# Layer 0's MLP: down products with the features on the partitions, and what follows from it

## The chip, the cores and the metric

One core of one Trainium2 chip runs the whole program. The metric is the device time of one execution in microseconds. Three runs of the kernel before gave 1023.16, 1023.51 and 1023.9 (median 1023.51).

## What is computed

Two layers of an encoder on x of 512 tokens by 1024 features, all in float32:

```
for layer in 0, 1:
    h = rms_norm(x, norm_mix[layer])
    x = x + (stick_breaking_attention(h) if layer == 0 else rglru_block(h))
    h = rms_norm(x, norm_mlp[layer])
    u = relu(h @ w1[layer])           # 512 x 4096
    x = x + (u * u) @ w2[layer]       # 512 x 1024
return rms_norm(x, norm_final)
```

The change concerns the second product of layer 0's MLP, called the down product, and the step from it to the first product of layer 1's mixer (`rglru_block`, weights `w_in`).

## The kernel before

**Layout.** Between the stages x lies transposed: eight chunks `x[c]` of 128 features (on the partitions) by 512 tokens. The chunks 0 to 3 are one half of the features, 4 to 7 the other.

**Exact products.** Every product is made of three: each operand is split into a high half (a cast to fp32r) and a low half (operand minus high half, also fp32r), and high times high, high times low and low times high are added up in PSUM. So each weight that arrives costs a cast on ScalarE (ACT), `wh`, and a subtraction on VectorE (DVE), `wl`. `halves` (L132 on) does the same for x times the norm's gain, into `xgh` and `xgl`.

**The MLP (class `Mlp`).** The 4096 hidden features are taken in four quarters. `quarters` first makes 1024 hidden features by plain products (`squared`); `run` then works through the list `steps`: 14 down steps for the first quarter, and for each further quarter 14 up steps and 14 down steps. Both use seven products of half-size blocks in place of eight (Winograd's scheme): `PRODUCTS` names them P1 to P7, with the block of the left operand, the block of weights, the block that is added to it before, the PSUM sum, the output quadrant and its sign. The order of the down steps is `ORDERS["mid"]`: P1 0, P5 0, P1 1, P2 0, P5 1, P6 0, P6 1, P3 0, P3 1, P7 0, P7 1, P2 1, P4 0, P4 1; the digit is the half of the quarter. In this document these are steps 0 to 13. Layer 1's MLP is the `mixed` one; layer 0's isn't.

**A down step before** (`part`, matmuls on L1190): the squared hidden values are the stationary operand (128 tokens), the weights move (512 features), so a PSUM bank holds 128 tokens by 512 features. There are 12 matmuls, first the 8 with `wh`, then the 4 with `wl`. `collect` takes a sum out of PSUM into a quadrant `c[out]`, multiplied on the way by the token's norm factor, which is one number per partition (`rr`, L1158). The quadrants: c0 and c1 belong to the first 256 tokens, c2 and c3 to the last 256; c0 and c2 to features 0 to 511, c1 and c3 to the others. P1 and P2 go into c0, P6 and P3 into c1, P4 into c2, P5 and P7 into c3, over all quarters.

**The end before.** `end` makes P4 of the last quarter by `times` (L1149). `feature` (L1518 on) turns a chunk back by four 128x128 transposes on TensorE (L1522) into PSUM, adds it to x (`add_x`, L765) and makes `xgh` and `xgl`. Chunks 4 to 7 come after the first half of P4, chunks 0 to 3 inside `beside`, which makes the first two `w_in` products. `Squares` gathers the squares for the next norm.

**What sets the order.** TensorE (PE) runs strictly in the order of the program. The other engines and the queues are ordered by a scheduler, except where the class `Ordered` wraps an engine: each instruction then comes after the one before it (`issue_after`). `Mlp` wraps V (DVE) and A (ACT), not G (GpSimd, POOL). All of these record L793. `prepare` makes the weights of a step about four steps ahead: `leave(i)`, called as the program comes to step i + 1, first collects the sum that step i completed, then prepares step i + 4. `operand` (L1109) makes `wh` and `wl`; there are four buffers of each, so a step's buffers are those of the step four earlier. `added` (L1127) makes the sums of weight blocks: P5 and P6 mostly on DVE, P7 and P4 by a transfer that adds in flight, issued on POOL's queue (L1131). In `operand`, UP_AT and OPEN_AT are small offsets in a buffer's row.

`x` itself is put away to DRAM while its tiles serve other ends (`between`), and `back` loads it again on SP's queue (L1547) as the last quarter's down steps begin.

The functions that the diff touches:

Of the kernel before, what the change touches and what calls it, by code (L numbers as in the profile page):

```python
# [18 lines left out]
P = 128  # L19
# [45 lines left out]
def hybrid_encoder(  # L65
# [81 lines left out]
    class Squares:  # L147
# [4 lines left out]

        def chunk(self, c, xc, last=None, pool=None, e=V):
            if not self.begun:
                self.begun = True
                self.acc = work.tile([P, S], F32, tag="r", name="ssq")
                A.activation(self.acc, xc, AF.Square)
            else:
                sq = (pool or work).tile([P, S], F32, tag="sq", name="sq")
                A.activation(sq, xc, AF.Square)  # L160
                with tc.issue_after(last.ins) if last else nullcontext():
                    self.last = e.tensor_tensor(self.acc, self.acc, sq, ALU.add)
# [640 lines left out]
    class Mlp:  # L803
# [323 lines left out]
        def added(self, unit, name, far=False):  # L1127

            _, b, to, *_ = self.PRODUCTS[name]
            if far or name in self.FAR:  # L1130
                G.dma_start(  # L1131
                    out=unit[b].rearrange("p j n -> p (j n)"), in_=unit["src"](to), accum_op=ALU.add
                )
# [41 lines left out]
        def part(self, sums, name, g, w):  # L1175
# [8 lines left out]
            if (name, g) == ("P1", 1):  # L1184
                rounds = ((h, wh),), ((h, wl),), ((l, wh),)
            for n, pairs in enumerate(rounds):
                for i in range(2):
# [13 lines left out]
        def run(self, first, between, end):  # L1201
# [42 lines left out]
            def make(i):  # L1244
# [3 lines left out]
                kind, q4, p, name = steps[i]  # L1248
                at = 0
                if kind == "up":  # L1250
                    at = self.OPEN_AT if i == 0 or (p, name) == (0, "P1") else UP_AT
                ws[i] = made[i] = self.operand(self.source(unit(i), name), at)

# [59 lines left out]
            def leave(i):  # L1313
# [5 lines left out]
                if kind == "down":  # L1319
# [124 lines left out]
            for i, (kind, q4, g, name) in enumerate(steps):  # L1444
# [12 lines left out]
                if new:  # L1457
                    banks[to] = self.bank()
                self.up(name, ws.pop(i), banks[to], new)
            for e in (self.V, self.A):  # L1460
                e.turn(False)
            end([ws[len(steps) - 2 + g] for g in range(2)], sums["down", NQ - 1, 0]["X"])

# [19 lines left out]
        def quarters(self, between, end):  # L1483
            for c in range(C - 1):
# [13 lines left out]
                if c == C - 2:  # L1498
                    self.rr = self.sq.inv_squares(self.bank())
                between(c)  # L1500

# [8 lines left out]
    with ExitStack() as mctx:  # L1510
# [6 lines left out]

        def feature(c, tag):  # L1518

            pt = bank(tag)  # L1520
            for t in range(NB):
                PE.transpose(  # L1522
                    pt[:, t * P : (t + 1) * P], mlp.y(t, c // 4)[:, c % 4 * P : (c % 4 + 1) * P],
                    ident,
                )
            add_x(c, pt)
            last["low"] = halves("mix1", c, x[c])
# [15 lines left out]

        def back():
            for c in range(C):
                x[c] = home_tile(*HOMES[c], "x")
                nc.sync.dma_start(out=x[c], in_=away[:, c, :])  # L1547

        end.ready = back
# [464 lines left out]
```

## Time and profile before

| | |
|---|---|
| median of three runs | 1023.51 us |
| the profiled execution | 1023.47 us |
| its span on the core | 1021.7 us |
| granted clock of TensorE, mean | 0.998 |
| the last quarter's down steps up to P4 | 520 to 552.7 us of the span |
| there: PE, DVE, ACT, POOL busy | 32.70, 31.25, 19.80, 3.49 us of 32.7 |
| P4, transposes and two `w_in` products | 552.7 to 572.5 us |
| there: PE, DVE, ACT, POOL busy | 19.80, 17.56, 13.56, 4.72 us of 19.8 |
| transfers of 512 KB that add, on POOL's queue | 66 in the MLPs, 10 in layer 1's mixer |

Times in rows are microseconds from the span's start; a row of a timeline has the start, the length, the engine, the line, the operation, what it writes and reads, and the count. In brackets stands the idle time before it and what ended it. The ends of matmuls are modelled, so the pace of PE is read from the starts. A row of the waits names the engine, who it waited for, the sum, the count and the longest. Issue to landing is counted from the start of the issuing instruction.

### The profile page before, as it was taken

Reading aid. Unit: us, or ns where it says so; the run is one execution under the profiler, and the core shown is the slowest. Engines: PE = TensorE matmul, PEld = TensorE weight load, DVE = VectorE, ACT = ScalarE, POOL = GpSimd, SP = SyncE. Lnnn points to the kernel's source line nnn. Section 1 sums busy time; section 2 is a strip of 40 time slices with the busy share of each in tenths; the row PEclk is TensorE's granted clock in tenths of the full one; section 3 lists DMA queues with packets and bytes.
Section 4 is the critical chain, followed back from the end, with each engine's and each line's share of the span. In section 5 each row is a group of like instructions: output and inputs, shape, how many; then the busy total and the mean of one; then the engine's idle time right before and its main releaser. Section 6 shows DMA issues by size and latency. Waiting matters only on the chain.

```text
span 1021.7 us, 16053 instructions
## 1 busy us (share of the span) xinstructions
PE 1013.0 (99%) x5930; PEld 890.1 (87%) x5930; DVE 868.3 (85%) x1165; ACT 701.5 (69%) x1081; POOL 175.5 (17%) x239
## 2 busy tenths in 40 slices
PE   9999999999999999999999999999999999999997
PEld 8888888888888988988988888888988988988986
DVE  7988787848789799799799888899898898898897
ACT  7777676835767764764775799966873763873866
POOL 0454344420000011011011221100010010010012
PEclk9999999999999999999999999999999999999999
DMA  7745454537536666676783476446767667667653
GB/s 237 222 122 145 115 152 102 152 111 262 160 81 198 166 156 195 166 158 194 166 230 90 118 192 173 116 170 200 214 112 206 165 143 202 173 142 201 168 106 111
DMA packets 58719, 165.73 MB, mean 162 GB/s; under 512 B 6928, under 2 KB 12304, under 8 KB 58640
## 3 DMA queue, kind: packets, MB, share of 16 engines
q1 hardware_dynamic: 47264, 124.41, 37.5%
q0 software_dynamic: 10944, 39.85, 23.4%
q8 instruction: 47, 0.77, 0.3%
q10 hardware_dynamic: 432, 0.44, 0.1%
q14 instruction: 32, 0.26, 0.1%
HBM read 140.56 MB, written 6.29 MB: 144 GB/s over the span
## 4 chain that ended last, share of the span: by engine, by line
PE 93%; ACT 3%; DVE 2%; DMA 1%; issue 1%; POOL 0%; ACTq 0%; DVEq 0%
PE ps_t L1190 16%; PE ps_acc L1055 9%; PE ps_acc L1190 9%; PE ps_z L1055 8%; PE ps_acc L234 5%; PE ps_acc L236 5%; PE ps_acc L235 5%; PE ps_o L1055 5%; PE ps_z L1190 4%; PE ps_t L234 2%; PE ps_t L236 2%; PE ps_t L235 2%; PE ps_o L234 2%; PE ps_o L236 2%; PE ps_o L235 2%; PE ps_t L628 2%
## 5 line engine op out<-in xcount | busy, mean ns | idle before, releaser
L793 ACT CAST wh<-b 128x1024 fp32r<-128x1024 f32 x174 | 180.3, 1051 | 121.6 <-DVE b L793 76.7
L793 DVE TENSOR_TENSOR wl<-b,wh 128x1024 fp32r<-128x1024 f32 x174 | 210.4, 1220 | 38.7 <-ACT wh L793 37.5
L1131 POOL DMA_DIRECT2D b<-in_w_dn x40 | 35.0, 875 | 295.3 <-DVE b L793 198.6
L234 PE MATMUL ps_acc<-xgh,wh 128*128 128x512 f32 x192 | 78.4, 408 | 0.0
L793 ACT ACTIVATE u<-u 128x512 f32<-128x512 f32 x103 | 64.9, 632 | 15.3 <-DVE u L793 13.5
L236 PE MATMUL ps_acc<-xgl,wh 128*128 128x512 f32 x192 | 75.2, 392 | 0.0
L235 PE MATMUL ps_acc<-xgh,wl 128*128 128x512 f32 x192 | 75.1, 391 | 0.0
L1131 POOL DMA_DIRECT2D b<-in_w_up x26 | 22.7, 872 | 291.7 <-DVE b L793 100.7
L606 DVE TENSOR_TENSOR_SCAN scan<-keep,later 128x128 f32<-128x128 f32 (+1 forms) x64 | 58.7, 918 | 15.4 <-POOL w L600 7.6
L793 DVE TENSOR_TENSOR b<-b,b 128x1024 f32<-128x1024 f32 x50 | 61.2, 1224 | 1.3
L610 POOL TENSOR_TENSOR w<-w,scan 128x128 f32<-128x128 f32 (+1 forms) x64 | 53.0, 830 | 53.4 <-DVE scan L606 48.8
L793 DVE TENSOR_TENSOR u<-u 128x512 f32<-128x512 f32 (+1 forms) x89 | 55.0, 618 | 4.4 <-ACT u L793 2.5
L229 DVE TENSOR_TENSOR wl<-raw,wh 128x512 fp32r<-128x512 f32 (+2 forms) x64 | 54.3, 877 | 4.1 <-ACT wh L227 4.0
L793 ACT CAST wh<-raw 128x1024 fp32r<-128x1024 f32 x49 | 51.2, 1048 | 6.8 <-PE ps_acc L1190 2.9
L227 ACT CAST wh<-raw 128x512 fp32r<-128x512 f32 (+2 forms) x64 | 44.4, 732 | 14.8 <-PE ps_acc L236 7.3
L1055 PE MATMUL ps_z<-xgh,wh 128*128 128x256 f32 x216 | 50.6, 277 | 0.2
L793 DVE TENSOR_TENSOR wl<-raw,wh 128x1024 fp32r<-128x1024 f32 x39 | 48.0, 1230 | 0.8 <-ACT wh L793 0.8
L1190 PE MATMUL ps_t<-wh,bh 128*128 128x512 f32 x120 | 47.0, 392 | 0.0
L1190 PE MATMUL ps_t<-wh,bl 128*128 128x512 f32 x120 | 46.8, 390 | 0.0
L600 POOL TENSOR_SCALAR_AFFINE_SELECT w<-w 128x128 f32<-128x128 f32 x64 | 32.9, 513 | 69.9 <-ACT w L595 69.7
L1055 PE MATMUL ps_acc<-low,wh 128*128 128x256 f32 x192 | 44.7, 276 | 0.0
L793 DVE TENSOR_TENSOR sl<-u,sh 128x512 fp32r<-128x512 f32 (+2 forms) x53 | 37.9, 716 | 7.7 <-ACT sh L793 7.7
(419 smaller groups left out, 3215.9 us busy)
## 6 DMA issues: line engine op xcount, KB each, us to landing
b<-in_w_dn SPq DMA_DIRECT2D x48, 512.0 KB, 4.3
b<-in_w_dn POOLq DMA_DIRECT2D x40, 512.0 KB, 5.6
b<-in_w_up SPq DMA_DIRECT2D x39, 512.0 KB, 4.6
b<-in_w_up POOLq DMA_DIRECT2D x26, 512.0 KB, 5.5
raw<-in_w_dn SPq DMA_DIRECT2D x16, 512.0 KB, 4.6
raw<-in_w_in SPq DMA_DIRECT2D x16, 512.0 KB, 3.7
raw<-in_w_up SPq DMA_DIRECT2D x13, 512.0 KB, 4.0
raw<-in_w_qk SPq DMA_DIRECT2D x12, 512.0 KB, 3.8
```

What stands on the lines that cost most here:

```text
L227: e[0].copy(wh[:, k, :], raw[:, k, :])
L229: e[1].tensor_tensor(wl[:, k, :], raw[:, k, :], f(wh[:, k, :]), ALU.subtract)
L234: PE.matmul(ps, wh, ah, start=start, stop=False)
L235: PE.matmul(ps, wl, ah, start=False, stop=False)
L236: PE.matmul(ps, wh, al, start=False, stop=stop)
L600: G.affine_select(t, t, pattern=[[-1, P]], compare_op=ALU.is_gt, fill=0.0, base=0, channel_multiplier=1,)
L606: V.tensor_tensor_scan(sc[:, S - n : S][:, ::-1], keep[:, :n][:, ::-1], later[:, S - n :][:, ::-1], 1.0, ALU.mult, ALU.max,)
L610: G.tensor_tensor(wt, wt, sc[:, S - n + 1 : S + 1], ALU.mult)
L793: ins = getattr(self.e, name)(*args, **kwargs)
L1055: PE.matmul(ps[:, i * HS : (i + 1) * HS], m, y, start=new and i == k == low == 0 and y is h, stop=(low, i, k) == steps[-1], skip_group_che ...
L1131: G.dma_start(out=unit[b].rearrange("p j n -> p (j n)"), in_=unit["src"](to), accum_op=ALU.add)
L1190: PE.matmul(sums[to][i], a[:, j, block, i * P : (i + 1) * P], y[:, j, :], start=new and g == j == n == 0 and a is h, stop=g == j == 1 and ...
```

## The change

For layer 0's MLP only:

- The down products are made by features (`across`, in `part` and at the end): the weights are the stationary operand (128 features), the squared hidden values move (256 tokens). A step is 24 matmuls of 256 columns, 16 with `wh`, then 8 with `wl`. The quadrants now hold two times 512 columns: for each 128 features, 256 tokens. So no transposes are needed. The offsets of the weights in their buffers change with their role.
- A token's factor is now different along the row. `collect` adds or subtracts without a factor; each quadrant is multiplied once, when its last sum is in, by a tile `rr` that holds the 512 factors on every partition. The factors are stored to DRAM (`keep_factors`) and loaded back, spread to all partitions, with x (`back`). The multiplications are on DVE (`times_factors`); P4's last sums are multiplied in PSUM.
- c2 (as it stands after P6) and c1 (after P3) are added to x by four transfers each, of 128 KB, that add in flight, on POOL's queue (`block`). c3 and c0, and P4's sums, are added by DVE.
- In the last quarter the low halves of six steps' weights (`ADDED`: steps 8 to 13) are no longer subtracted on DVE: ACT writes minus the high half into `wl`, and a transfer on POOL's queue adds the raw weights to it.
- GpSimd's transfers of layer 0's MLP are wrapped by `Ordered` as well, so they are issued in the order of the program.
- The operations after P4 (high and low halves of x, squares) are written out in a fixed order on DVE and ACT; the squares go through the ordered ACT.

The core of the diff:

```diff
-            self.V, self.A = Ordered(V), Ordered(A)
+            self.V, self.A, self.G = Ordered(V), Ordered(A), Ordered(G)
+            self.G.turn(not self.mixed)
...
+        ADDED = (("P7", 0), ("P7", 1), ("P3", 1), ("P2", 1), ("P4", 0), ("P4", 1))
+
-        def operand(self, raw, at):
+        def operand(self, raw, at, added=False):
...
             self.A.copy(wh, raw)
-            self.V.tensor_tensor(wl, raw, f(wh), ALU.subtract)
+            if added:
+                self.A.activation(wl, f(wh), AF.Copy, scale=-1.0)
+                self.G.dma_start(out=wl, in_=raw, accum_op=ALU.add)
+            else:
+                self.V.tensor_tensor(wl, raw, f(wh), ALU.subtract)
             return wh, wl
...
-                G.dma_start(
+                self.G.dma_start(
                     out=unit[b].rearrange("p j n -> p (j n)"), in_=unit["src"](to), accum_op=ALU.add
                 )
...
+        def across(self, name, g, i, w, ps, new=False, ends=True, rounds=None):
+
+            block = self.PRODUCTS[name][0]
+            (wh, wl), (h, l) = w, self.a[g]
+            rounds = rounds or [((h, wh), (l, wh)), ((h, wl),)]
+            for n, pairs in enumerate(rounds):
+                for jj in range(2):
+                    for a, y in pairs:
+                        for k in range(2):
+                            f0 = (2 * i + k) * P
+                            PE.matmul(
+                                ps[:, k * HS : (k + 1) * HS], y[:, jj, f0 : f0 + P], a[:, jj, block, :],
+                                start=new and n == jj == k == 0 and a is h,
+                                stop=ends and (n, jj, k) == (len(rounds) - 1, 1, 1),
+                                skip_group_check=name not in ("P1", "P5", "P2"),
+                            )
...
+            if not self.mixed:
+                if (out, i) in self.begun:
+                    op = ALU.subtract if less else ALU.add
+                    self.gained = self.V.tensor_tensor(y, y, ps, op)
+                else:
+                    self.begun.add((out, i))
+                    A.activation(y, ps, AF.Identity, scale=1.0 - 2.0 * less)
+                return
...
+                added = kind == "down" and q4 == NQ - 1 and not self.mixed
+                ws[i] = made[i] = self.operand(
+                    self.source(unit(i), name), at, added and (name, p) in self.ADDED
+                )
...
                     if p:
                         for n in range(2):
                             self.collect(name, n, bank[n])
+                        if not self.mixed and q4 == NQ - 1:
+                            end.done(name)
                     if not ahead:
                         prepare_or_hold(i)
...
+        def block(out):
+            h, ts = out % 2, (lo, hi)[out // 2]
+            times_factors(mlp.V, mlp.c[out].rearrange("p i n -> p (i n)"), ts)
+            for k in range(4):
+                mlp.G.dma_start(
+                    out=x[4 * h + k][:, ts],
+                    in_=mlp.c[out][:, k // 2, k % 2 * HS : (k % 2 + 1) * HS], accum_op=ALU.add,
                 )
+        def done(name):
+            if name == "P6":
+                block(2)
+            elif name == "P3":
+                block(1)
+            elif name == "P7":
+                times_factors(mlp.V, mlp.c[3].rearrange("p i n -> p (i n)"), hi)
+            elif name == "P2":
+                add_block(mlp.V, 3)
+                times_factors(mlp.V, mlp.c[0].rearrange("p i n -> p (i n)"), lo)
...
         def end(ws, xs):
             for i in range(2):
                 for g in range(2):
-                    mlp.times("P4", g, i, ws[g], xs[i], False)
-                mlp.collect("P4", i, xs[i])
-                if i == 0:
-                    for c in range(4, C):
-                        feature(c, "zzoo"[c - 4])
-                        squares.chunk(c, x[c], e=G)
+                    mlp.across("P4", g, i, ws[g], xs[i], ends=g == 1)
...
+            high(4, 5, 6, 7)
+            low(4, 5)
+            add_block(mlp.V, 0, range(2))
+            low(6, 7)
+            square(4, 5)
+            times_factors(mlp.V, xs[0], hi)
+            add_last(0)
+            high(0)
+            square(6)
+            high(1)
+            times_factors(mlp.V, xs[1], hi)
+            add_block(mlp.V, 0, range(2, 4))
+            add_last(1)
+            low(0, 1)
+            square(7)
+            high(2, 3)
+            low(2, 3)
...
         beside(
-            [slab(w_in[C + i]) for i in range(2)], xgh, xgl, begin,
-            {
-                1: lambda: [feature(c, "z") for c in range(2)],
-                2: lambda: [feature(c, "o") for c in range(2, 4)],
-            },
-            (*range(4, C), *range(4)),
+            [slab(w_in[C + i]) for i in range(2)], xgh, xgl, begin, {}, (*range(4, C), *range(4)),
         )
```

`high` and `low` make `xgh` and `xgl` of chunks on the ordered ACT and DVE; `add_block` adds a quadrant's parts to x on DVE; `add_last` adds P4's sums.

More of the change, by code (lines that the diff above doesn't have):

```diff
@@ L1459, in run @@
                 self.up(name, ws.pop(i), banks[to], new)
+            rest = [ws[len(steps) - 2 + g] for g in range(2)], sums["down", NQ - 1, 0]["X"]
+            if not self.mixed:
+                end(*rest)
             for e in (self.V, self.A):
                 e.turn(False)
-            end([ws[len(steps) - 2 + g] for g in range(2)], sums["down", NQ - 1, 0]["X"])
+            if self.mixed:
+                end(*rest)
         def mixed_quarters(self, residues, gains, end):
@@ L1499, in quarters @@
                     self.rr = self.sq.inv_squares(self.bank())
+                    between.factors(self.rr)
                 between(c)
@@ L1516, in hybrid_encoder, with keep_factors @@
         last = {}
[L1518 to L1524, printed above, removed]
-                )
-            add_x(c, pt)
-            last["low"] = halves("mix1", c, x[c])
+        factors = dram.tile([1, S], F32, tag="factors", name="factors")
+        lo, hi = slice(0, HS), slice(HS, S)
+        rr = []
+        def keep_factors(cols):
+            nc.sync.dma_start(
+                out=factors.rearrange("o (t p) -> p (o t)", p=P), in_=cols[:, :NB]
+            )
@@ new lines, in back, with times_factors @@
+        def back():
+            for c in (*range(4), *range(4, C)):
+                x[c] = home_tile(*HOMES[c], "x")
+                nc.sync.dma_start(out=x[c], in_=away[:, c, :])
+                if c == 0:
+                    rr.append(mlp.mp.tile([P, S], F32, tag="low", name="rr", bufs=1))
+                    nc.sync.dma_start(out=rr[0], in_=factors.broadcast_to([P, S]))
+        def times_factors(e, y, ts):
+            n = y.shape[1] // HS
+            y = y.rearrange("p (k n) -> p k n", k=n)
+            e.tensor_tensor(y, y, rr[0][:, ts].unsqueeze(1).broadcast_to([P, n, HS]), ALU.mult)
@@ L1529, in end, with low, square @@
+        def low(*cs):
+            for c in cs:
+                last["low"] = mlp.V.scalar_tensor_tensor(
+                    xgl[:, c, :], x[c], col("mix1")[:, c : c + 1], f(xgh[:, c, :]),
+                    ALU.mult, ALU.subtract,
+                )
+        def square(*cs):
+            for c in cs:
+                squares.chunk(c, x[c], e=G, a=mlp.A)
         def end(ws, xs):
@@ L1542, in between @@
                 soft.send(mlp.ready)
[L1544 to L1549, printed above, removed]
+        between.factors = keep_factors
+        end.ready, end.done = back, done
         mlp.quarters(between, end)
```

33 lines of the change are left out of this document (27 added, 6 removed).

## Prediction

> **What bounds the kernel now.** I read the page's busy times first, then PE's waits, then the chain of waits around the end of layer 0, then the timelines of ACT, DVE, POOL and the DMA queues there. Page, part 1, and the whole list of PE's waits:
>
> ```profile
> PE 1013.0 (99%) x5930; PEld 890.1 (87%) x5930; DVE 868.3 (85%) x1165; ACT 701.5 (69%) x1081; POOL 175.5 (17%) x239
> PE ps_z L396 <- DVE dense_ones L118: 1.1, 1, 1.1
> PE ps_z L587 <- ACT keep L596: 0.2, 1, 0.2
> ```
>
> PE is never let wait: two waits, 1.3 us, in the whole span. So any matmul time taken out shortens the kernel, and any operand that comes late lengthens it, one for one. The chain at the end of layer 0's last down quarter (start, length, what):
>
> ```profile
> 517.23 2.72 PE ps_z L1055 x24
> 519.95 2.75 PE ps_t L1190 x12
> ...
> 550.02 2.72 PE ps_z L1190 x12
> 552.74 2.72 PE ps_t L1149 x12
> 555.46 0.87 PE ps_z L1522 x8
> 556.34 0.87 PE ps_o L1522 x8
> 557.21 2.75 PE ps_t L1149 x12
> 561.32 0.87 PE ps_z L1522 x8
> 563.58 0.87 PE ps_o L1522 x8
> ```
>
> Each of the fourteen down steps is 12 matmuls of 512 columns in 2.72 us (I number them 0 to 13: 8 is P3 1, 9 and 10 are P7 0 and 1, 11 is P2 1, 12 and 13 are P4 0 and 1). L1522 are the transposes.
>
> **Matmuls.** The change turns a step into 24 matmuls of 256 columns. The row of 24 (L1055, the up product) and the row of 12 both last 2.72 us, each matmul with a weight load of its own, so the price is nothing in the row. The Trainium skill, "TensorE: Matmul & The Clock Gate", section "Back-to-back issue gap", speaks against it: it gives the gap as N/2.4 + 2.5 ns, so 672 more matmuls (4 quarters x 14 steps x 12) would add an estimated 1.7 us; the trace's equal rows do not bear that out, and it stays out of the sum.
>
> **Transposes.** They go. Timeline of PE, the first matmul of step 8, of P4, and the first matmul after the two w_in products (48 matmuls of 512):
>
> ```profile
> 541.70 0.39 PE L1190 MATMUL ps_acc<-wh,sh 128*128 128x512 f32 x1
> 552.58 0.39 PE L1149 MATMUL ps_t<-wh,bh 128*128 128x512 f32 x1
> 572.50 0.39 PE L234 MATMUL ps_t<-xgh,wh 128*128 128x512 f32 x1
> ```
>
> 552.58 to 572.50 is 19.92 us; the 24 + 48 matmuls that stay need 72 x 2.72/12 = 16.32. Removed: 3.6 us, all of it on the path.
>
> **Row multiplications, adds and the end on DVE.** Collecting keeps its operations (one pair per product, 1.41 us below, now without a scale). New: four products by the factors, eight adds of 256 columns, the two last PSUM blocks; gone: eight adds of x, two collects, six low halves. Timeline of DVE (the 277.74 row is the price of a 256-column operation, the pitch of following ones 0.34):
>
> ```profile
> 277.74 0.42 DVE L793 TENSOR_TENSOR x<-x 128x256 f32<-128x256 f32 x1
> 278.08 0.42 DVE L793 TENSOR_TENSOR low<-x,s 128x256 fp32r<-128x256 f32 x1
> 537.97 1.41 DVE L793 SCALAR_TENSOR_TENSOR c<-ps_acc,rr,c 128x512 f32<-128x512 f32 x2
> 541.02 0.68 DVE L793 TENSOR_TENSOR sl<-u,sh 128x512 fp32r<-128x512 f32 x1
> 542.76 1.41 DVE L793 SCALAR_TENSOR_TENSOR c<-ps_t,rr,c 128x512 f32<-128x512 f32 x2
> 545.21 1.22 DVE L793 TENSOR_TENSOR wl<-raw,wh 128x1024 fp32r<-128x1024 f32 x1
> 546.35 1.41 DVE L793 SCALAR_TENSOR_TENSOR c<-ps_acc,rr,c 128x512 f32<-128x512 f32 x2
> 547.66 2.35 DVE L793 TENSOR_TENSOR wl<-b,wh 128x1024 fp32r<-128x1024 f32 x2
> 549.93 1.41 DVE L793 SCALAR_TENSOR_TENSOR c<-ps_t,rr,c 128x512 f32<-128x512 f32 x2
> ```
>
> If PE never stalled, it would reach chunk 0 of the w_in products at 552.58 + 5.44 + 5.44 = 563.5 and need its low half 0.45 later. Before that half DVE has, from 549.93: two collects (2.6), two products by the factors (2.3), the two w_in low halves (2.3), eight adds (2.7), two PSUM products (1.3), four PSUM adds (1.4), four low halves (2.6), by pitches 1.31, 1.14, 0.34 and 0.66: 15.2 us, and the half itself 0.75. That is 565.9, 2.0 us late. Where PE has stalled 2 us or more after step 10, this costs nothing; the next late thing is then the transfers.
>
> **The six low halves.** Now the wait that I think decides. A low half was one DVE operation straight after ACT's cast; now ACT casts, ACT writes the negative, and POOL issues a transfer that adds the raw weights. ACT around it, the negative's price from the same operation in layer 1's mixer, POOL's transfers of this kind there, and the last weight transfer ahead on POOL's queue with its landing:
>
> ```profile
> 534.60 2.00 ACT L793 CAST wh<-b 128x1024 fp32r<-128x1024 f32 x2 [4.01 <-DVE b L793]
> 536.51 0.61 ACT L793 CAST sh<-u 128x512 fp32r<-128x512 f32 x1
> 537.03 1.05 ACT L793 CAST wh<-b 128x1024 fp32r<-128x1024 f32 x1
> 578.56 1.06 ACT L793 ACTIVATE wl<-wh 128x1024 fp32r<-128x1024 f32 x1
> ```
> ```profile
> L1639 POOL DMA_DIRECT2D wl<-raw x10: 855/886/908, 580.0 to 650.6; - x10
> DMA to landing us min/median/max: 4.5/6.1/7.9
> ```
> ```profile
> 537.32 0.88 POOL L1131 DMA_DIRECT2D b<-in_w_dn  x1 [3.97 <-DVE wl L793]
> DMA to landing us min/median/max: 5.4/5.4/5.4
> ```
>
> The cast at 537.03 is step 8's; it can't come earlier, since ACT's order is written out and the two casts before it waited for DVE's sum (b in the first row), which the change leaves where it is. The negative ends near 539.0, the transfer is issued at 539.1. PE wants the low half two thirds into the step: 541.70 + 1.81 = 543.5. The fastest of ten landings gives 543.6, the median 545.2. So step 8 stalls by 0.1 to 1.7 at least, before any queueing.
>
> Queueing: two issues of the same quarter that follow each other on POOL's queue, each with its landing, and the page's two queues:
>
> ```profile
> L1131 POOL DMA_DIRECT2D b<-in_w_dn x1: 875/875/875, 518.4 to 518.4; - x1
> DMA to landing us min/median/max: 8.1/8.1/8.1
> L1131 POOL DMA_DIRECT2D b<-in_w_dn x1: 865/865/865, 520.7 to 520.7; - x1
> DMA to landing us min/median/max: 8.2/8.2/8.2
> q1 hardware_dynamic: 47264, 124.41, 37.5%
> q0 software_dynamic: 10944, 39.85, 23.4%
> ```
>
> They landed at 526.5 and 528.9, 2.4 apart. POOL's 39.85 MB took 23.4% of 16 engines' 1021.7 us: 3.15 us for 0.52 MB, against 1.6 on SP's queue. So adding transfers of 512 KB follow each other at 2.4 to 3.15 us, beside steps of 2.72, and the change puts six of them and eight of 128 KB (0.6 to 0.8 each, by bytes) into one line.
>
> POOL's order is now written out too. After step 6 DVE collects P6 and multiplies c2 (the collect, at 542.76 before, moves up, as two low halves of weights leave DVE ahead of it: from 537.97, a pair of 1.3 and two low halves of u at 0.6 end near 540.5, P6's pair near 541.7, the product by the factors near 542.8); then POOL issues four transfers to x, which at 0.88 each hold it until 546.3. ACT, at 1.0 for a cast or a negative and 0.5 for a sh, has step 9's negative at 541.4, which still goes ahead of them, and step 10's at 543.3, which is queued behind them. After P3, four more hold it from 548.8 to 552.3, and P4's two low halves are issued at 552.3 and 553.2.
>
> With the rule "4.5 us after issue, and no sooner than the spacing after the one before", starting from 542.7 (537.3 + 5.4), at spacing 2.4: step 8 lands at 545.1 (stall 1.6); step 9 at 547.5, wanted 546.2 + 1.6, none; the blocks at 549.9; step 10 at 552.3, wanted 548.95 + 1.6 (stall 1.75); step 11 in time; blocks 557.1; P4 0 at 559.5, wanted 553.5 + 3.35 (2.65); P4 1 at 561.9, wanted 554.85 + 6.0 (1.05): 7.1 us in all. At 3.15 the same walk gives 2.3, 0.45, 3.55, 0.45, 4.45 and 1.8: 13.0. I take the middle, 10.1, since the one spacing is a single pair and the other a mean with other traffic in it. DVE's end is then covered.
>
> **Small things at nothing.** The factors' store goes out on SP's queue in layer 0's first products, their broadcast with the reload of x ahead of the last down steps; both are first used after step 6. ACT's six negatives are in the issue times above. Layer 1's mixer starts from PE's stream and moves with it. The new offsets of the weights are those that the up products have, at full rate. If these covers fail: under 1 us together, either way.
>
> **The sum.** -3.6 + 10.1 = +6.5 on the profiled execution's 1023.47 us (span 1021.7 and 1.8 around it; median of the runs 1023.51): 1030.0, with 1026.9 to 1032.9 as this case's own range (-3.6 + 7.1 to -3.6 + 13.0).
>
> **Rivals.**
> - *The transfers land in time, so it is faster.* If an adding transfer needs at most 4.4 us, side by side with others, and a 128 KB one keeps POOL for a quarter of 0.88, then step 8 is met at 543.5, step 10's is issued at 543.7 and lands at 548.1 before 548.95, and P4's are early. Left are -3.6 and up to 2.0 for DVE's end: 1019.9 to 1021.9. For it: no transfer in the trace of before made PE wait. Against it: ten landings, none under 4.5. Here the Trainium skill, "DMA: Bandwidth & Descriptors", section "Anatomy of one DMA", stands on this side: 2.0 us + bytes/436e3 gives an estimated 3.2 us for 512 KB. The trace disagrees, 4.5 to 7.9. Chance 0.25 (0.2 of it beyond 0.2%).
> - *No queueing, only the order.* Each transfer takes its median 6.1 us and none delays another, POOL still works through its order: stalls of 1.7 at step 8, 1.8 at step 10 (issue 546.35), 1.4 at P4: 4.9 - 3.6 = +1.3, 1024.8. For it: engines often stand idle there. Against it: the pair 2.4 apart. Chance 0.2, of which 0.05 goes over 0.2%.
> - The forecast: 0.55.
>
> **The numbers.** A difference under 0.2% (2.05 us) can't be told from none by these runs. Faster 0.2, same 0.05 + 0.15 = 0.2, slower 0.55 + 0.05 = 0.6. The range reaches from inside the first rival to just above the forecast's upper end: 1020.5 to 1033.5, with about 0.1 left out on each side.
>
> **What would show it.** In the profile after: 24 matmuls of 256 columns still 2.72 us; no L1522 transposes; PE waits, for the first time, on a transfer of wl, at step 8 (about 1.7 us), step 10 and P4; POOL's rows with four issues of about 0.88 between the low halves; landings of wl growing from 6 to 8 us and more. I am wrong if PE's list of waits stays empty there, if the 128 KB issues are short, or if adding transfers overlap. If PE waits on xgl of chunk 0 instead, the DVE sum was the bound.

## The result, and the profile after

The changed kernel takes 1036.53 us (median of 4 executions, 1035.74 to 1038.01) beside 1023.34 us for the kernel before in the same series (4 executions, 1022.57 to 1023.90): 1.0131 times as long, 95% interval 1.0114 to 1.0149. The prediction said 1030.0 us, in a range of 1020.5 to 1033.5. Its direction was right, and its mechanism (TensorE waits for low halves that come by transfers) too; the time lies 3 us above the range. The profiled execution took 1038.01 us, 14.54 more than that of before.

TensorE's busy time and POOL's queue, from the page of the changed kernel:

```profile
PE 1013.0 (98%) x6570; PEld 917.2 (89%) x6570; DVE 864.1 (83%) x1167; ACT 706.8 (68%) x1087; POOL 185.8 (18%) x253
q0 software_dynamic: 12960, 44.05, 25.4%
```

TensorE is busy for the same 1013.0 us as before, in a longer span, so the span grew by waiting. (That the two are equal is chance: the 3.6 us of the transposes went, and products at half pace, below, came.) The view of waits of the changed kernel, from 500 to 600 us (total, times, longest), where before had none:

```profile
PE ps_t L1157 <- DMA wl<-b: 12.3, 2, 8.4
PE ps_acc L1157 <- DMA wl<-b: 1.9, 1, 1.9
```

The timeline of TensorE in the same run tells where (start, length, in brackets the idle time before and what ended it):

```profile
544.94 1.19 PE L1157 MATMUL ps_acc<-sh,wl 128*128 128x256 f32 x8 [1.91 <-DMA wl<-b]
554.55 2.08 PE L1157 MATMUL ps_t<-sh,wl 128*128 128x256 f32 x8 [3.89 <-DMA wl<-b]
569.25 1.22 PE L1157 MATMUL ps_t<-bh,wl 128*128 128x256 f32 x4 [8.44 <-DMA wl<-b]
587.47 0.39 PE L234 MATMUL ps_t<-xgh,wh 128*128 128x512 f32 x1
```

These are step 8, step 10 and P4 0, the three steps that the prediction named: 14.2 us. The last row is the product that stood at 572.50 before: 14.97 later. The windows of the changed kernel (busy us and count of PE, PEld, DVE, ACT and POOL; then PEclk, the DMA engines' share and GB/s):

```profile
555.00:560.00 5.00, 5.00 (x35) 5.00 (x35) 4.03 (x5) 0.97 (x1) 3.26 (x4) 0.73 0.98 184
560.00:565.00 5.00, 0.81 (x8) 0.61 (x6) 5.00 (x9) 2.03 (x4) 0.96 (x2) 0.95 1.10 261
565.00:570.00 5.00, 0.75 (x3) 0.76 (x4) 2.74 (x6) 1.76 (x3) 1.30 (x1) 0.50 0.93 236
570.00:575.00 5.00, 5.00 (x26) 4.98 (x25) 1.45 (x3) 0.13 (x1) 0.00 (x0) 0.53 0.02 4
```

Behind the waits of 3.89 and 8.44 us the granted clock (0.73, 0.50, 0.53) is down for a while. The 40 products after P4 0's wait take 569.25 to 576.56, 7.3 us, where 40 x 2.72/24 is 4.5; the 16 after step 10's take 3.4 instead of 1.8. The prediction had no term for that.

The timeline of POOL in the changed kernel (all its work there is issuing transfers):

```profile
539.02 0.87 POOL L793 DMA_DIRECT2D wl<-b  x1 [1.38 <-ACT wl L793]
...
542.72 0.87 POOL L793 DMA_DIRECT2D x<-c  x1 [0.26 <-issue]
545.20 0.86 POOL L793 DMA_DIRECT2D x<-c  x1 [1.61 <-issue]
547.68 1.77 POOL L793 DMA_DIRECT2D x<-c  x2 [1.62 <-issue]
549.06 1.29 POOL L793 DMA_DIRECT2D wl<-b  x1
...
557.43 1.76 POOL L793 DMA_DIRECT2D x<-c  x2 [1.74 <-issue]
559.11 0.97 POOL L793 DMA_DIRECT2D wl<-b  x1
562.07 0.88 POOL L793 DMA_DIRECT2D wl<-b  x1 [1.99 <-issue]
```

The small transfers to x were taken to be issued 0.88 apart. They come 2.5 to 3.1 apart in several places (551.72 and 554.81 in the part left out), with POOL idle in between, and P4's two halves go out at 559.1 and 562.1, not at 552.3 and 553.2.

For the experiments I use two lengths. *The section* runs from the first product of layer 0's last down quarter to the first product of layer 1's third column of weights (572.50 before, 587.47 after): 52.7 us before, 68.5 after. *The two quarters* run from the first product of the second down section to that of the last one, at 366.28 and 519.78 before: 153.5 us before, 152.8 after. With -0.8 for what lies ahead of the section, +15.8 for it and -0.4 for what follows, the profiled executions' 14.5 is accounted for.

### The profile page after: what moved, and what is told of

The parts are those of the page before. It is cut to its first block, busy times and chain, and to the rows that moved or that the text cites. A ratio compares the mean times of both kernels' runs of the same rounds, so it can differ in the third digit from the quotient of the medians.

```text
span 1036.3 us, 17382 instructions
## 1 busy us (share of the span) xinstructions
PE 1013.0 (98%) x6570; PEld 917.2 (89%) x6570; DVE 864.1 (83%) x1167; ACT 706.8 (68%) x1087; POOL 185.8 (18%) x253
## 4 chain that ended last, share of the span: by engine, by line
PE 87%; ACT 3%; DVE 3%; DMA 2%; issue 2%; POOL 1%; POOLq 0%; ACTq 0%; DVEq 0%
PE ps_acc L1056 9%; PE ps_t L1230 8%; PE ps_z L1056 7%; PE ps_t L1157 7%; PE ps_acc L234 5%; PE ps_acc L236 5%; PE ps_acc L235 5%; PE ps_acc L1230 4%; PE ps_o L1056 4%; PE ps_acc L1157 3%; PE ps_t L234 2%; PE ps_t L236 2%; PE ps_t L235 2%; PE ps_z L1230 2%; PE ps_o L234 2%
## 5 line engine op out<-in xcount | busy, mean ns | idle before, releaser
L793 DVE TENSOR_TENSOR wl<-b,wh 128x1024 fp32r<-128x1024 f32 x169 | 204.3, 1219 | 39.8 <-ACT wh L793 38.5
L606 DVE TENSOR_TENSOR_SCAN scan<-keep,later 128x128 f32<-128x128 f32 (+1 forms) x64 | 58.9, 921 | 15.8 <-ACT keep L596 8.1
L793 DVE TENSOR_TENSOR u<-u 128x512 f32<-128x512 f32 (+1 forms) x89 | 54.9, 617 | 4.4 <-ACT u L793 2.5
L595 ACT ACTIVATE w<-ps_z,rp 128x128 f32<-128x128 f32 (+3 forms) x56 | 29.7, 531 | 20.9 <-PE ps_z L588 17.0
L236 PEld LDWEIGHTS ps_acc<-xgl,wh 128*128 128x128 f32 x192 | 36.0, 188 | 7.8
```

Of the source, the lines that this page charges most:

```text
L236: PE.matmul(ps, wh, al, start=False, stop=stop)
L606: V.tensor_tensor_scan(sc[:, S - n : S][:, ::-1], keep[:, :n][:, ::-1], later[:, S - n :][:, ::-1], 1.0, ALU.mult, ALU.max,)
L793: ins = getattr(self.e, name)(*args, **kwargs)
```

## The experiments

All are edits of the changed kernel, except where another base is named. Ratios are to the kernel before on the same chip.

| run | what is different | median us (executions) | ratio, 95% interval | two quarters | section |
|---|---|---|---|---|---|
| changed kernel | | 1036.53 (4) | 1.0131, 1.0114 to 1.0149 | 152.8 | 68.5 |
| E1 | no half by transfer | 1024.63 (10) | 1.0021, 1.0004 to 1.0038 | 152.8 | 54.3 |
| E2 | additions to x on VectorE | 1029.85 (5) | 1.0064, 1.0040 to 1.0089 | 152.8 | 59.2 |
| E3 | both | 1027.87 (8) | 1.0044, 1.0030 to 1.0058 | 152.8 | 57.1 |
| E4 | 1536 bytes for descriptors | 1040.26 (4) | 1.0159, 1.0130 to 1.0188 | 158.0 | 67.2 |
| E5 | three halves, c2's transfers last | 1025.28 (10) | 1.0014, 0.9993 to 1.0034 | 158.0 | 53.7 |
| E6 | three halves | 1029.85 (4) | 1.0064, 1.0046 to 1.0082 | 152.8 | 59.7 |
| E7 | six halves, c2's transfers last | 1036.61 (4) | 1.0121, 1.0097 to 1.0145 | 158.0 | 61.2 |
| E8 | E1 with idle time filled | 1026.89 (8) | 1.0033, 1.0011 to 1.0054 | 152.8 | 54.8 |
| E9 | changed kernel, idle time filled | 1041.34 (5) | 1.0179, 1.0159 to 1.0200 | 152.8 | 67.3 |
| E10 | three halves, c2 on VectorE, other order | 1030.20 (6) | 1.0062, 1.0045 to 1.0078 | 158.0 | 54.3 |
| E11 | none | 1041.58 (5) | 1.0179, 1.0165 to 1.0193 | 158.3 | 65.8 |
| E12 | E5 with four products of 512 columns | 1029.59 (5) | 1.0053, 1.0040 to 1.0066 | 155.8 | 54.9 |

The last two columns are of the profiled execution. The two quarters take 152.8 or some 158 us in kernels whose instructions there are the same. This is a matter of its own (E11 and E12), and it moves single executions by 5 to 7 us. So I compare the sections, and times only where the two quarters agree. The section is not free of it either: the changed kernel's is 68.5 us in one series and 65.8 in the other (E11), so between runs whose two quarters differ, a difference of sections is uncertain by some 3 us.

My theory at the outset: the low halves come late, because the transfers of 512 KB follow one another on POOL's queue behind the small ones, and the clock falls after the long waits. The rivals: the layout and the work on VectorE cost the time; or POOL's limit of transfers in flight does.

### E1 to E3: which part costs the time

E1 sets `ADDED = ()`. E2 replaces the transfers to x:

```
-            for k in range(4):
-                mlp.G.dma_start(
-                    out=x[4 * h + k][:, ts],
-                    in_=mlp.c[out][:, k // 2, k % 2 * HS : (k % 2 + 1) * HS], accum_op=ALU.add,
-                )
+            add_block(mlp.V, out)
```

E3 does both.

> The six low halves go back to VectorE's subtraction; layout, row multiplications and the eight transfers to x stay. Theory A (matmuls wait for late low halves, and the clock falls behind the long waits): both waits go, the section keeps the 3.6 us of the transposes and the 0.65 us before it, less 0 to 4 us that the six subtractions of 1.14 us cost VectorE at the section's end: 1019 to 1024 us. Theory B (the layout, the row multiplications and the order written out cost the time): above 1030 us, with other waits on TensorE's list.

> The eight additions of 128x256 to x are made by VectorE (2.9 us at 0.36 each); the six low halves stay adding transfers. Theory C (what makes the halves late is above all that they stand behind the eight small transfers on POOL's queue): steps 10 and P4 0 stop waiting, step 8 still waits 2 us, 1021 to 1026 us. Theory D (an adding transfer of 512 KB is too slow for its step by itself, 5 to 6 us from issue to landing each, one after another at 2.7 to 3.2 us): waits at three or more steps, 1027 to 1033 us.

> No adding transfer at the end of layer 0's MLP: six subtractions and eight additions on VectorE (6.8 + 2.9 us more there). Theory A: no wait on transfers, 1019 to 1024 us, within 1.5 us of the run without the low halves alone; if VectorE's sum then sets the end, TensorE waits for xgl or x at layer 1's mixer and it is 1024 to 1030 us. Theory B: above 1030 us.

E1: 1024.63 us; 14.2 us of the section are gone, all of the waits for low halves. So the halves cost it, not the layout (Theory B falls). The median lies 0.6 us above A's range, with three of the ten executions at 1028.6 to 1030.3. And E1 isn't faster than before. Its timeline of TensorE at layer 1's first products:

```profile
560.28 0.50 PE L234 MATMUL ps_acc<-xgh,wh 128*128 128x512 f32 x1 [2.23 <-ACT xgh L793]
561.75 0.63 PE L235 MATMUL ps_acc<-xgh,wl 128*128 128x512 f32 x1
562.18 0.63 PE L236 MATMUL ps_acc<-xgl,wh 128*128 128x512 f32 x1
```

TensorE waits 2.2 us for xgh, which waits for VectorE's sums in x, and then takes 0.43 per product instead of 0.23. So VectorE's end takes back the 3.6 us of the transposes. E3 has no wait for a transfer either, and its section is 2.9 us longer than E1's, about the 8 x 0.36 that VectorE adds; its 1027.87 us is the case of A in which VectorE's sum sets the end. Its waits:

```profile
PE ps_t L1157 <- DVE c L793: 2.6, 1, 2.6
PE ps_acc L236 <- DVE xgl L793: 1.5, 2, 1.2
```

E2's 1029.85 us lies in D's range. Its timeline of TensorE tells more:

```profile
544.91 1.21 PE L1157 MATMUL ps_acc<-sh,wl 128*128 128x256 f32 x8 [1.69 <-DMA wl<-b]
556.16 0.74 PE L1157 MATMUL ps_t<-bh,wl 128*128 128x256 f32 x4 [0.39 <-DMA wl<-b]
561.84 1.22 PE L1157 MATMUL ps_t<-sh,wl 128*128 128x256 f32 x4 [4.04 <-DMA wl<-b]
```

With the small transfers gone, the wait at step 10 is gone and P4 0's falls from 8.44 to 0.39: the section is 9.3 us shorter. So C is right in that the place behind the small transfers cost most of it, and D in that three waits remain without them. The rows also give the pitch of the 512 KB transfers by themselves: from step 8's landing at 544.91 to P4 0's at 556.16 four of them land, 2.8 us each on average. The third wait isn't this pitch: P4 1's half, issued at 553.28, lands 5.7 us behind P4 0's, with no other transfer on POOL's queue, while two loads of layer 1's weights, issued at 553.7 and 554.1, run on SP's.

### E4: more room for descriptors

```
-    nc = _bacc.Bacc("TRN2", target_bir_lowering=False, num_devices=1, dynamic_dma_scratch_size=1024)
+    nc = _bacc.Bacc("TRN2", target_bir_lowering=False, num_devices=1, dynamic_dma_scratch_size=1536)
```

> The same instructions in the same order; only the memory for descriptors of POOL's transfers grows from 1024 to 1536 bytes. Theory E (POOL holds at most three transfers in flight for want of that memory, and this delays the issue of P4's halves): issues move up, four or five in flight, the wait at P4 0 falls from 8.4 to 1 to 4 us, 1026 to 1033 us. Theory F (the data of the transfers run one after another at the engines' rate, so that earlier issue only lengthens the time to landing): issues move up, landings don't, 1035 to 1038 us.

The issues moved up as both theories said. POOL's timeline of E4, step 8's half, the first three transfers to x, and P4's two halves:

```profile
544.41 0.87 POOL L793 DMA_DIRECT2D wl<-b  x1 [1.30 <-ACT wl L793]
548.11 2.65 POOL L793 DMA_DIRECT2D x<-c  x3 [0.26 <-issue]
...
561.80 1.77 POOL L793 DMA_DIRECT2D wl<-b  x2 [1.64 <-issue]
```

So that memory is what spaced them. E4's time, above both ranges, can't be set beside 1036.53, since its two quarters took 158.0; E11, the changed kernel at 158.3, is its partner. There step 8's half is issued at 546.26 and P4 0's at 566.52, 20.3 later; in E4 17.4 later. The products that waited for P4 0's half, first E4's, then E11's:

```profile
571.81 1.22 PE L1157 MATMUL ps_t<-bh,wl 128*128 128x256 f32 x4 [6.35 <-DMA wl<-b]
```
```profile
574.27 1.21 PE L1157 MATMUL ps_t<-bh,wl 128*128 128x256 f32 x4 [4.94 <-DMA wl<-b]
```

From step 8's issue that is 27.4 us in E4 and 28.0 in E11. Issued 2.9 earlier, landed 0.6 earlier: for this half the data decide, not the issue. Theory E falls, F stands, though not with this queue's data alone: in both runs loads on SP's queue begin some 10 us ahead of this landing (561.6 in E4, 564.5 in E11). The waits on transfers add up to 10.9 and 10.7 us.

### E5 to E7: how many halves, and in which order

E5 adds only `(("P7", 0), ("P7", 1), ("P2", 1))` and issues c2's four transfers last (on P6 only the product by the factors stays; `block(2)` without it opens `end`). E6 has these three halves in the change's own order. E7 has all six, in E5's order.

> Three low halves by adding transfers (P7 of both groups and P2 of group 1), three on VectorE; the four transfers of c2 to x are issued last, behind all halves. Without any half on POOL, TensorE lost 2.4 us to VectorE's sum and 2.4 us to the clock after it. Theory A (each half must have some 6 us between issue and need, and VectorE must be 3 us ahead): VectorE does 3.4 us less than there, no half is late: 1019 to 1022 us, faster than before. Theory D (an adding transfer of 512 KB is too slow for its step): waits at two of the three steps, 1023 to 1027 us.

> The same three halves, with the transfers to x in the change's own order: c2's four stand ahead of P7 1's and P2 1's halves on POOL's queue. Theory C (the place behind the small transfers makes halves late): TensorE waits 2 to 4 us at P7 1, and the clock falls with the longer ones, 1022 to 1027 us, 2 us or more above the run with c2's transfers last. Theory A without an order effect: the same within 1 us, 1019 to 1022 us.

> The whole change, six halves and eight transfers, with c2's four small ones issued last instead of ahead of P7 1. Theory C: P7 1 no longer waits (4.1 us), P4 0 waits at most 4 us less than its 8.4, what is left are step 8's 2 us and the waits of P4: 1026 to 1032 us. Theory F (the data of the transfers, in any order, are too much for the queue): 1033 to 1038 us.

E6 against E5 isolates the order: 59.7 against 53.7 us, at different paces. The wait itself doesn't depend on the pace: E6's timeline of TensorE has one for a half, step 10's, which stands behind four small transfers (first row); E5 has none for a half, and its only wait from 500 to 600 us is for VectorE (second row, from the view of waits):

```profile
554.43 2.07 PE L1157 MATMUL ps_t<-sh,wl 128*128 128x256 f32 x8 [5.03 <-DMA wl<-b]
```
```profile
PE ps_acc L236 <- DVE xgl L793: 2.8, 1, 2.8
```

So Theory C holds, at a price larger than I expected (5.0 instead of 2 to 4 us of wait, and 1029.85 us above the range). Here the issue is what is late: POOL issues E6's half at 549.74, when the small transfers have gone out, and it lands 4.6 us later. E5 isn't faster than before, as I had expected it to be: 1.0014, with 1 in the interval; the median lies in D's range, though no half is late. Its ten executions fall into 1021.24 to 1023.17 (five) and 1027.39 to 1028.41 (five); the profiled one, 1028.41, has the two quarters at 158.0. What the others had isn't known.

E7 keeps the transfers to x of c1 ahead of P4's halves. Step 10 no longer waits, step 8 (first row) and P4 0 still do:

```profile
550.47 1.20 PE L1157 MATMUL ps_acc<-sh,wl 128*128 128x256 f32 x8 [0.51 <-DMA wl<-b]
569.38 1.22 PE L1157 MATMUL ps_t<-bh,wl 128*128 128x256 f32 x4 [8.34 <-DMA wl<-b]
```

Its section is 61.2 us, 4.6 less than E11's at the same pace. Its time, 1036.61, lies in F's range and above C's, but with 5.2 us of the slower pace in the profiled execution it can't decide between them; E11, at the same pace, took 1041.58.

### E8 and E9: is the clock on the path

In E8, on E1's base, ten products of 512 columns that nobody reads stand ahead of layer 1's first; in E9 16 and 36 of them stand between the products by wh and by wl of step 10 and of P4 0:

```
+            spare = bank("o")
+            for _ in range(10):
+                PE.matmul(
+                    spare.rearrange("p (b n) -> p b n", b=2), ws[1][0][:, 0, :P],
+                    mlp.a[1][0][:, 0, :2, :], start=True, stop=True,
+                )
```

> As the run without any half on POOL, with ten multiplications of 128x512 whose sums nobody reads between P4's last product and layer 1's first: they fill the 2.4 us in which TensorE waits for xgh. Theory G (TensorE's clock falls because it stood idle, and this costs as much again as the wait): the pace of 0.43 us per product after the wait goes back to 0.23, 2 to 2.5 us less, 1021.8 to 1022.8 us. Without that theory: 1024.2 to 1025 us, the same as without them.

> The whole change; between the products by wh and by wl of P7 1 and of P4 0, where TensorE waited 4.1 and 8.4 us, stand 16 and 36 multiplications of 128x512 whose sums nobody reads (3.6 and 8.2 us). Theory G (the long waits lower the granted clock afterwards, and in the whole change, where VectorE has 5 us to spare, this reaches the end): the 3.9 us of half pace go, 1031.5 to 1033.5 us. Without it: 1035.5 to 1038 us. The landings of the halves stay where they are in both.

The windows from 560 to 565 us, E1's and then E8's, and from 565 to 570 of E9 (0.50 in the changed kernel):

```profile
560.00:565.00 5.00, 4.66 (x12) 3.40 (x13) 4.70 (x10) 3.45 (x7) 1.49 (x1) 0.66 0.03 7
```
```profile
560.00:565.00 5.00, 5.00 (x23) 3.99 (x22) 4.96 (x9) 2.69 (x5) 1.51 (x1) 1.00 0.01 3
```
```profile
565.00:570.00 5.00, 5.00 (x25) 4.09 (x24) 5.00 (x7) 2.33 (x4) 1.90 (x1) 1.00 1.06 262
```

So idle time is what lowers the clock: filled, it stays at 1.00. The Trainium skill, "TensorE: Matmul & The Clock Gate", Part 1, has a rule of this kind: half rate after an idle window of some 3.4 us, the window running free. The waits of 3.89 and 8.44 us agree with it; E1's wait of 2.2 us, shorter than that window, lowered the clock as well. But the expected gain came in neither. E8's section is 54.8 us, against 54.3: with the clock at full, TensorE arrives sooner and waits 1.8 us for xgl. (Its median, 1026.89, says nothing: four executions took 1023.0 to 1024.9, four 1028.9 to 1030.6.) E9's is 67.3 us, 1.2 less than the changed kernel's. There the added products end at 569.64, 0.8 after P4 0's half has landed, and the timeline of TensorE then has a new wait, for P4 1's half:

```profile
572.14 0.74 PE L1167 MATMUL ps_t<-sh,wl 128*128 128x256 f32 x4 [0.97 <-DMA wl<-b]
```

P4 1's half lands at 571.9 in the changed kernel and at 572.1 in E9; only what follows it can gain, and what half pace cost before it had lain over the wait. The median of E9, 1041.34, says nothing on this, since its executions fall into two groups, 1036.88 (the profiled one) and 1041.22 to 1045.45.

### E10: VectorE's last order

E10 has E5's three halves, c2's additions on VectorE, and xgl of chunks 0 and 1 ahead of P4's second pair:

```
             high(1)
+            low(0, 1)
             times_factors(mlp.V, xs[1], hi)
             add_block(mlp.V, 0, range(2, 4))
             add_last(1)
-            low(0, 1)
```

> Three halves by adding transfers as before (P7 of both groups, P2 1), c2's four additions to x on VectorE in the 2 us that it stood idle there, and the low halves of xg's chunks 0 and 1 made right after their last sum, ahead of P4's second pair. Theory H (what is left of the loss without late halves is the order of VectorE's last 15 us: TensorE waited 2.8 us for xgl of chunk 0): no wait above 1 us at layer 1's first products; 1018.5 to 1021 us in executions in which layer 0's products keep the 113 ns pace and 6 to 7 us more in those at 118 ns, the median 1019 to 1023 us. Theory D: a half is late still, 1023 to 1027 us.

No half is late (Theory D falls), and neither is xgl of chunk 0. The timeline of TensorE has the wait two chunks on:

```profile
576.45 0.50 PE L234 MATMUL ps_acc<-xgh,wh 128*128 128x512 f32 x1 [2.27 <-ACT xgh L793]
```

So Theory H falls too, and the median, 1030.20, lies above both ranges: this order only moved the wait. That the amount of VectorE's work behind P4 sets the end fits E3, whose added work lengthened the section, but no other order was tried. In E5 a part is something else: two additions of VectorE took 2.24 us at 568.58, where such a pair takes 0.75; why isn't known. The section, 54.3 us, stays 1.6 above before's.

### E11 and E12: two paces

E11 is the changed kernel again. E12 is E5 with one product of 512 columns that nobody reads in each down section, after the products by wh of P7 1.

> The changed kernel once more, unedited, for the spread of its executions: in other kernels of this study single executions of layer 0's MLP kept a pace of 118 ns per product of 256 columns instead of 113 from about 385 us on and took 5 to 7 us more. Theory K (the pace comes with the layout by features, so the changed kernel has it too): executions in two groups, 1035 to 1038 and 1039 to 1044 us, the median wherever the larger group is. Theory L (it comes with single edits): all within 1034.5 to 1038.5 us.

> The kernel with three halves by adding transfers and c2's transfers last (1021.2 to 1023.2 us in five executions, 1027.4 to 1028.4 in five), with one multiplication of 128x512 that nobody reads in each of layer 0's four down sections, at P7 of group 1 (0.9 us in all). Theory M (a pace of 118 ns ends at the next product of another width): the slow spell ends some 8 us after 385 us, no execution above 1025 us, median 1022 to 1024 us. Theory N (it ends only at a wait, or never by such a product): the two groups stay, 1022 to 1024 and 1028 to 1030 us.

E11 took 1040.82 to 1044.49 us, 1041.58 in the median: 5 us more than the first series, with the same instructions. One window of each, the changed kernel's first profile and E11's:

```profile
480.00:520.00 40.00, 40.00 (x356) 40.00 (x355) 31.82 (x32) 29.91 (x40) 3.58 (x5) 1.00 0.70 184
```
```profile
480.00:520.00 40.00, 40.00 (x342) 40.00 (x341) 31.33 (x32) 25.75 (x32) 3.48 (x4) 1.00 0.62 139
```

TensorE is busy throughout, the granted clock is 1.00 in both, and 356 products of 256 columns go by in one and 342 in the other: 112 and 117 ns each (113 and 118 within a step). Theory K holds, with the first series as its quicker group and E11's as its slower one; L falls. E12's windows, each in another quarter, with one of the four added products between any two:

```profile
370.00:397.00 27.00, 27.00 (x232) 27.00 (x231) 26.18 (x32) 16.51 (x21) 2.93 (x4) 1.00 0.80 189
410.00:440.00 30.00, 30.00 (x268) 30.00 (x267) 23.38 (x24) 23.68 (x30) 2.17 (x3) 1.00 0.70 162
490.00:520.00 30.00, 30.00 (x258) 30.00 (x257) 24.96 (x25) 23.43 (x31) 1.75 (x2) 1.00 0.70 176
```

116, 112 and 116 ns: the pace changes at each of these products, in both directions (the quarter ahead of 319 us, where the first one stands, is quick). So M is half right, the other width does change it, but it doesn't end the slow pace; N's mechanism falls, though all five executions, 1028.1 to 1029.8, lie in its slower group. Down products of 512 columns, as before had them, show 227 ns in all four of its quarters.

No kernel here beats the one before beyond doubt: E5's five quicker executions are 0.5 to 2.4 us below before's median of 1023.66, the others 3.7 to 4.8 above. I found nothing that holds the quick pace.

## Why the prediction was wrong

- **Direction and mechanism: right.** TensorE waits for low halves at step 8, step 10 and P4 0, and E1 takes these waits away and 14.2 us of the section with them.
- **The step that failed is the end of the walk of the six low halves ("blocks 557.1; P4 0 at 559.5"), with the line that put nothing against it: "Layer 1's mixer starts from PE's stream and moves with it".** The walk gives POOL's queue the same spacing to its end.

  Up to 558.8 us that held. The 512 KB transfers were sized well: 2.4 to 3.15 was said, 2.8 measured in E2. The small ones too: 0.6 to 0.8 was said, and where they land right behind another transfer it is 0.6 to 1.0 (landings at 547.4, 548.1, 548.7; 557.1, 557.8, 558.8). From step 8's landing at 544.9 to 558.8, 13.9 us, three halves and six small transfers land, which the prediction's sizes put at 10.8 to 14.25. Step 8 waits 1.91 (said: 1.6 to 2.3), step 10 3.89 (1.75 to 3.55).

  Behind 558.8 the last two small transfers and P4 0's half come 2.9, 3.9 and 3.6 us apart, 10.4 where 3.6 to 4.75 was said, and P4 0 waits 8.44 (2.65 to 4.45). The changed kernel's answers on these issues; the last one covers the last small transfer, issued at 558.1 (7.5), and P4 0's half (10.1):

```profile
L793 POOL DMA_DIRECT2D x<-c x1: 877/877/877, 554.8 to 554.8; - x1
DMA to landing us min/median/max: 4.0/4.0/4.0
L793 POOL DMA_DIRECT2D x<-c x1: 872/872/872, 557.4 to 557.4; - x1
DMA to landing us min/median/max: 4.3/4.3/4.3
L793 POOL DMA_DIRECT2D wl<-b x1: 973/973/973, 559.1 to 559.1; - x1
DMA to landing us min/median/max: 7.5/8.8/10.1
```

  In that stretch SP's queue loads layer 1's weights over the same engines. Its timeline before, then its timeline and its list of waits in the changed kernel, and the DMA view there from 558 to 563 us:

```profile
528.01 18.77 SPq L221 DMA_DIRECT2D raw<-in_w_in  x2
```
```profile
527.16 30.34 SPq L221 DMA_DIRECT2D raw<-in_w_in  x2
558.51 26.69 SPq L1735 DMA_DIRECT2D raw<-in_w_in  x4
SPq L221 <- DMA wl<-raw: 29.6, 1, 29.6
```
```profile
q1 hardware_dynamic: 276, 1.01, 69.8%
q0 software_dynamic: 269, 0.26, 32.6%
```

  A row reaches from its first issue to the end of its last one, so the second load of the first row went out at 546.5 before, when VectorE had made step 11's low half and the raw weights' buffer was free. Now the adding transfer of that half reads the buffer until it lands at 557.1; the load goes out at 557.2, and the next at 558.5 and 562.0. From 558 to 560 us POOL's queue moved 0.01 MB and SP's 0.39, after 0.31 on POOL's in the 2 us ahead. So the change itself put the first of these loads beside P4's halves, and the others run there too. In E2, E4, E7 and E11, too, the load goes out as step 11's half lands. No run took the loads away, so their price is read from the traces, not shown by an experiment. P4 1's own wait (1.05 to 1.8 said) is hidden: its half lands at 571.9, and TensorE needs it at 571.97.
- **POOL's order: right as a place, wrong as a price.** The issues were put 0.88 apart; they came up to 3.1 apart, for want of memory for descriptors. E4 shows that this costs P4 0's half next to nothing, since its landing stayed. What costs is the place behind the small transfers: 5.0 us of wait for the one half that is late in E6.
- **The clock: not in the sum.** Behind the two long waits 56 products take 4.3 us more than at full pace, and -3.6 + 14.2 + 4.3 = 14.9 is near the 14.5 measured. Most of it lies over the waits for P4's halves: behind P4 1's landing the last 28 products take 4.6 us in the changed kernel and 3.3 in E9. So 1.2 to 1.3 us is a cost of its own.
- **The matmuls: "the price is nothing in the row" held for one of two paces.** At the quick one the two quarters take 152.8 us, 0.7 less than before; at the other 158.0. The estimate of 1.7 us from the Trainium skill, "TensorE: Matmul & The Clock Gate", section "Back-to-back issue gap", half of which would fall into these two quarters, fits neither. In the first series the changed kernel's profile shows the quick pace, so this isn't in the 14.5 us; it is the 5 us more of E11.
- **Transposes: right.** From 576.56 to 587.47 stand 48 products and nothing else, 10.9 us. VectorE's end "2.0 us late" where TensorE doesn't stall: right in kind. With the halves back on VectorE (E1) or with three of them (E5, E10) TensorE waits 2.2 to 2.8 us, and these waits, with the clock behind E1's, take back what the transposes gave: the sections are 53.7 to 54.3 us beside 52.7 before.
- The first rival (landings within 4.4 us) falls: the six halves land 5.4 to 10.1 us after issue. No run's median reaches its 1019.9 to 1021.9 us, but three of E5's executions do (1021.2 to 1021.5). The second rival (no queueing) falls by E2: a transfer delays the next by 2.8 us.

## What to carry to other kernels

Before work is moved from a busy engine to adding transfers, add up the queue that they share, with the other traffic of that stretch, and compare it with the time between the first and the last need: here 24.3 us lay between step 8's and P4 0's landings, where TensorE wanted them 10 us apart (543.5 and 553.5 in the prediction). Ask also what a transfer holds while it runs: here one adding transfer gave its source buffer free 10.7 us later than VectorE had, and so moved the next layer's load into the stretch of P4's halves. Put the transfer that a matmul waits for ahead of those that only need to land some time. And where work is cut from a busy TensorE, ask which engine is next: here VectorE, 2 to 3 us behind, took what the transposes had given.

## What the runs showed of the hardware

- Products of 256 columns, with the granted clock at 1.00, run at 112 or at 117 ns each, in the same program from one execution to the next and for up to 180 us at a stretch (E5); each of E12's four single products of 512 columns switched from one pace to the other. Other switches fell on hand-overs between two steps with a gap of 0.2 to 0.4 us. What the two states are isn't settled.
- Waits of 1.9 us (E9, step 8), 2.2 (E1) and 2.6 (E3) were followed by half pace; others of 1.9 us (the changed kernel, step 8), 2.3 (E10) and 2.8 (E5) were not.
- 1024 bytes of memory for descriptors hold POOL's issues back to one in 2.5 to 3.1 us once a few transfers are under way; 1536 bytes let three go out in 2.65 us.
- In the changed kernel a transfer of 128 KB that was issued in time lands 0.6 to 1.0 us behind the one ahead of it while only POOL's queue moves data, and 2.9 and 3.9 us behind it beside loads on SP's queue.
